# Split projection weights kept in DRAM by the first block, and the elementwise chain spread over the r and v units

## The chip, the cores and the metric

The kernel runs on one core of one Trainium2 chip. The metric is the time of one execution on the device in microseconds (us). One execution of each kernel is also recorded by the hardware profiler. Engines are named as in the profile: PE is TensorE (PEld its weight loads), DVE is VectorE, ACT is ScalarE, POOL is GpSimd, SP is SyncE, which here only issues DMAs.

## What is computed

Two layers on 2048 latent tokens with 256 context tokens as a prefix, 1024 channels: a bidirectional RWKV-7 mixer, then latent attention, each with modulated norms, a gate and a residual. The change is inside the projections of the RWKV mixer:

```python
def rwkv_prepare(h, mu, w_in, w0, w1, w2, a0, a1, a2, k_k, k_a):
    xx = centred_shift(h)
    lerp = lambda j: h + xx * mu[j]
    r = heads(lerp(0) @ w_in[0])
    k = heads(lerp(1) @ w_in[1])
    v = heads(lerp(2) @ w_in[2])
    gate = lerp(3) @ w_in[3]
    ...
    logw = heads(-jnp.exp(-jax.nn.softplus(-wpre) - 0.5))
    a = heads(jax.nn.sigmoid(...))
    kk = ...  # k * k_k, normalised per head
    k_dir = k[None] * (1.0 + (a - 1.0) * k_a.reshape(RWKV_HEADS, RWKV_HEAD))
    b = kk[None] * a
    return r, logw, k_dir, v, -kk, b, gate
```

`wpre` and `a` are there once for each of two directions; everything downstream of them is done twice.

## The kernel before

`run` goes through parameters, `project`, `scan` and `attention`. `project` calls `project_block` for five blocks of tokens: the context (256 columns, block 0) and four of 512 (blocks 1 to 4). Channels lie on partitions, in 8 tiles (index f for outputs, k for inputs); tokens are columns.

The large products run in split precision. `lerp_split(j)` makes the 8 input tiles of `lerp(j)` (L480) and parts each into a rounded half `lh` (L492, ACT) and the rest `ll` (L493, DVE, or POOL for odd k with j of 0 and 1). `load_w` does the same to a weight tile `wraw` of 128x1024: `whi` is a cast on ACT (L414), `wlo` the difference (L418), on POOL or parted between DVE and POOL by `DVK`, `DVR` and `DVV`. `mm3` then issues 24 matmuls (L500 to L502). All 24 tiles (k, r, v, 8 each) are loaded from the input and split again in every block. `w_seq` gives the order of the loads; one load runs ahead.

A block of 512 columns has these stretches: 16 fp32 matmuls for the low-rank hidden layers (L520); the **k units**, 8 times `load_w`, `mm3`, copies and a lerp kept for the gate; the **r units**, 8 times `mm3`, and for each two **halves** (direction d of 0 and 1); the **v units**, 8 times `mm3`, transposes and stores, with the norm of the next block (`pr_norm`) and steps of a small triangular solve (L1002, L1006, blocks 1 and 2) between them. In block 0 each v unit follows its r unit.

A half takes 4 matmuls `w2` (L602, L603) into `ps_l`, two tanh on ACT (`sg`, `ta`), then on DVE `sg`+1 (L610), a scan along the tokens (L613), two exponentials on ACT (`E`, `Ei`), and products that make `ar` (L622, L623, DVE), `kd` (L627, POOL), the first part of `kb` (L630, POOL), `ta` (L631, DVE) and the second part of `kb` (L632, DVE). `ar` and `kb` are stored by SP, 512 KB each; 32 small matmuls `ab` (L641) use them. Once for each f DVE makes `kkh` (L591) and `bt` (L657), and POOL adds the two `kd` (L655).

The order on each engine is set by the framework's scheduler from this program and from the buffers of its pools; engines run their own lists in order and wait for one another by semaphores. SP issues nearly all DMAs, in one list.

Of the kernel before, what the change touches and what calls it, by code (L numbers as in the profile page):

```python
# [19 lines left out]
P = 128  # L20
# [101 lines left out]
class Build:  # L122
# [194 lines left out]
    def project(self):  # L317
# [3 lines left out]
        with ExitStack() as es:  # L321
# [4 lines left out]
            tags = itertools.cycle(((wp, "whi"), (wp, "wlo"), (tp, "ar")))  # L326

            def modw():
                pool, tag = next(tags)
                return pool.tile([P, D], F32, name="modw", tag=tag, bufs=2)  # L330

            mg = self.mod_gen([(0, 0, 512, D)], 5, tp, pp, modw, "ps_l", {"tag": "kkh"})
# [10 lines left out]
            self.w_raw = next(self.w_it)  # L343
# [47 lines left out]
    def w_seq(self, wp):  # L391
        nc, ins = self.nc, self.ins
        for t0, _ in BLOCKS:
            for w1 in ("rwkv_w1", "rwkv_a1"):
                raw = wp.tile([P, KT, P], F32, name="wraw")
                for d in range(2):
                    nc.sync.dma_start(raw[:, :, d * 64:(d + 1) * 64], ins[w1][0, d].rearrange("(k p) m -> p k m", p=P))
                yield raw
            order = [(1, f) for f in range(KT)]
            order += [(j, f) for j in (0, 2) for f in range(KT)] if t0 else [(j, f) for f in range(KT) for j in (0, 2)]  # L400
            for j, f in order:
                raw = wp.tile([P, KT, P], F32, name="wraw")
                nc.sync.dma_start(raw, ins["rwkv_w_in"][0, j, :, f * P:(f + 1) * P].rearrange("(k p) m -> p k m", p=P))
                yield raw

    def next_raw(self):
        cur, self.w_raw = self.w_raw, next(self.w_it, None)
        return cur

    def load_w(self, wp, dv=0):  # L410
        nc = self.nc
        raw = self.next_raw()
        hi = wp.tile([P, KT, P], F32R, name="whi")
        nc.scalar.copy(hi, raw)  # L414
        lo = wp.tile([P, KT, P], F32R, name="wlo")
        for eng, k0, k1 in ((nc.vector, 0, dv), (nc.gpsimd, dv, KT)):
            if k1 > k0:
                eng.tensor_tensor(lo[:, k0:k1, :], raw[:, k0:k1, :], hi[:, k0:k1, :].bitcast(F32), ALU.subtract)  # L418
# [52 lines left out]
    def project_block(self, t0, W, bp, wp, tp, pp, ind, indt, smask, w2d, sol):  # L471
# [6 lines left out]
        def lerp(j, k):  # L478
            L = tp.tile([P, 512], F32, name="lerp", bufs=4)
# [3 lines left out]
        def lerp_split(j, into=None):  # L483
            lh, ll = [], []
            for k in range(KT):
# [3 lines left out]
                else:  # L489
                    h = bp.tile([P, 512], F32R, name="lh", bufs=10)  # L490
                    l = bp.tile([P, 512], F32R, name="ll", bufs=9)
                nc.scalar.copy(h[:, :W], L[:, :W])  # L492
                (nc.gpsimd if k % 2 and j != 2 else nc.vector).tensor_tensor(l[:, :W], L[:, :W], h[:, :W].bitcast(F32), ALU.subtract)  # L493
# [19 lines left out]
        DVK, DVR, DVV = (5, 0), (2, 0), (5, 3)  # L513
        HS = []
        for j in (4, 5):
            raw = self.next_raw()
            ps = pp.tile([P, 512], F32, name="ps_r")
            for k in range(KT):
                L = lerp(j, k)
                nc.tensor.matmul(ps[:, :W], raw[:, k, :], L[:, :W], start=k == 0, stop=k == KT - 1)  # L520
# [13 lines left out]
        for f in range(KT):  # L534
            hi, lo = self.load_w(wp, DVK[t0 > 0])
# [21 lines left out]
        def v_unit(f, lh, ll):  # L557
# [4 lines left out]
            hi, lo = self.load_w(wp, DVV[t0 > 0])  # L562
# [18 lines left out]
        bts = []  # L581
        abq = []
        for f in range(KT):
            hi, lo = self.load_w(wp, DVR[t0 > 0])
            if f == 0:
                w2 = load_w2(0)
            pi = pp.tile([P, 512], F32, name="ps_i", bufs=1)
            nc.tensor.matmul(pi[:, :W], indt[:, f, :], ivh[:, :W], start=True, stop=False)
# [1330 lines left out]
```

## Time and profile before

| | |
|---|---|
| runs | 5359.62, 5360.29, 5380.01 us; median 5360.29 us |
| profiled execution | 5361.62 us, its span 5359.8 us |
| mean granted TensorE clock | 0.92 of full speed |
| busy over the span | PE 86%, DVE 70%, POOL 54%, ACT 40% |
| the projection | from the start to about 1322 us |

The span is what the profiler saw from the first to the last instruction; 1.8 us lie around it. Busy shares are means over stages with different limits. The projection has its own pattern, which is why the rows below are taken from stretches of it.

### The profile page before, as it was taken

The page shows a single profiled execution, that of the slowest core. Times are in us where ns is not written, and L with a number is a line of the kernel's source. Part 1 is how long each engine was busy: PE and PEld are TensorE (multiplying, and loading weights), DVE is VectorE, ACT ScalarE, POOL GpSimd, SP SyncE. Part 2 cuts the span into 40 slices and gives each one's busy share as a digit, 9 for nine tenths or more (in the row PEclk, how much of TensorE's full clock was granted, in tenths as well). Part 3 has the DMA queues.
Part 4 walks back from the last instruction along what each step waited for, and adds up shares of the span by engine and source line. Part 5 has one row for each costly group of instructions (what it writes and reads, how often), then busy time and mean ns, then how long its engine had stood idle before and what let it go on. Part 6 is the DMA issues. An engine that isn't in the chain of part 4 may idle for free. (4 is left out here: it accounts for less than half of the span.)

```text
span 5359.8 us, 122473 instructions
## 1 busy us (share of the span) xinstructions
PE 4623.4 (86%) x50175; PEld 3437.2 (64%) x50175; DVE 3726.7 (70%) x6054; ACT 2167.4 (40%) x3830; POOL 2885.2 (54%) x2539
## 2 busy tenths in 40 slices
PE   6788788887878888677879999869999999999999
PEld 4555555555667777556757777746666666666667
DVE  5989898886788888777655544336666776666634
ACT  4544444443444444333433334214343434343332
POOL 2575656464454444434244444227777777777751
PEclk8898888888889899788979999979999999999999
DMA  7655464646776666877878777761111111211023
GB/s 220 190 167 174 151 182 153 188 152 188 211 219 183 182 175 182 219 212 223 243 228 259 240 216 192 237 213 34 60 58 33 57 54 34 60 58 34 27 94 107
DMA packets 1006877, 818.53 MB, mean 153 GB/s; under 512 B 280885, under 2 KB 876420, under 8 KB 994794
## 3 DMA queue, kind: packets, MB, share of 16 engines
q1 hardware_dynamic: 872046, 734.48, 46.0%
q10 hardware_dynamic: 134188, 75.95, 5.2%
q8 instruction: 394, 6.46, 0.5%
q14 instruction: 169, 1.38, 0.1%
q0 software_dynamic: 80, 0.26, 0.0%
HBM read 551.84 MB, written 258.66 MB: 151 GB/s over the span
## 5 line engine op out<-in xcount | busy, mean ns | idle before, releaser
L1724 POOL TENSOR_TENSOR acc<-acc,pt 128x1024 f32<-128x1024 f32 x416 | 1003.1, 2411 | 356.3 <-ACT pt L1712 333.6
L1712 ACT ACTIVATE pt<-ps_s 128x1024 f32<-128x1024 f32 x576 | 590.9, 1027 | 890.3 <-PE ps_s L1710 882.8
L1690 DVE TENSOR_REDUCE mx<-ps_p 128x1 f32<-128x512 f32 x1024 | 659.6, 686 | 258.6 <-PE ps_p L1686 258.6
L1731 PE MATMUL ps_o<-pt,av 128*64 128x512 f32 x2304 | 514.0, 595 | 0.0
L1710 PE MATMUL ps_s<-qr,a_kr 64*128 64x512 f32 (+1 forms) x2304 | 474.2, 392 | 0.3 <-DVE qr L1701 0.2
L418 POOL TENSOR_TENSOR wlo<-wraw,whi 128x1024 fp32r<-128x1024 f32 (+3 forms) x120 | 261.7, 2181 | 299.7 <-ACT whi L414 290.0
L500 PE MATMUL ps_r<-lh,whi 128*128 128x512 f32 (+1 forms) x960 | 384.6, 403 | 38.0 <-ACT lh L492 34.7
L501 PE MATMUL ps_r<-ll,whi 128*128 128x512 f32 (+1 forms) x960 | 381.6, 399 | 16.5 <-DVE ll L493 13.4
L502 PE MATMUL ps_r<-lh,wlo 128*128 128x512 f32 (+1 forms) x960 | 378.4, 396 | 15.0 <-DVE wlo L418 7.6
L696 POOL TENSOR_TENSOR f_wlo<-f_wraw,f_whi 128x384 fp32r<-128x384 f32 x118 | 159.3, 1350 | 388.6 <-ACT f_whi L694 339.8
L1731 PEld LDWEIGHTS ps_o<-pt,av 128*64 128x64 f32 x2304 | 159.5, 137 | 315.5 <-issue 315.5
L1686 PE MATMUL ps_p<-knh,qnh 64*128 64x512 f32 (+1 forms) x1280 | 274.7, 399 | 37.4 <-DMA qnl<-qn 33.3
L480 DVE SCALAR_TENSOR_TENSOR lerp<-xx,cols,hb 128x512 f32<-128x512 f32 (+1 forms) x240 | 239.2, 1022 | 86.1 <-POOL ll L493 65.9
L1150 PE MATMUL ps_s<-svu,big 128*64 128x64 f32 x4544 | 235.3, 247 | 50.9 <-DVE svu L1138 27.8
L1110 ACT COPY big<-ps_aa 64x256 f32<-64x256 f32 x576 | 211.0, 366 | 131.0 <-PE ps_aa L1106 125.0
L1097 DVE TENSOR_TENSOR big<-ps_aa,amask 64x256 f32<-64x256 f32 x576 | 243.0, 422 | 28.5 <-PE ps_aa L1092 15.0
L1686 PE MATMUL ps_p<-a_kr,qr 64*128 64x512 f32 (+1 forms) x1280 | 260.4, 379 | 1.7 <-DMA qr<-qr 1.7
L1710 PEld LDWEIGHTS ps_s<-qr,a_kr 64*128 64x128 f32 (+1 forms) x2304 | 235.2, 185 | 38.4 <-DVE qr L1701 0.5
L500 PEld LDWEIGHTS ps_r<-lh,whi 128*128 128x128 f32 x960 | 197.7, 206 | 92.3 <-ACT lh L492 39.4
L1710 PE MATMUL ps_s<-qnh,knl 64*128 64x512 f32 x1152 | 241.0, 402 | 12.2 <-ACT pt L1712 12.0
L1150 PEld LDWEIGHTS ps_s<-svu,big 128*64 128x64 f32 x4544 | 193.9, 156 | 86.0 <-DVE svu L1138 40.9
L501 PEld LDWEIGHTS ps_r<-ll,whi 128*128 128x128 f32 x960 | 198.0, 206 | 59.6 <-DVE ll L493 19.7
(343 smaller groups left out, 12357.4 us busy)
## 6 DMA issues: line engine op xcount, KB each, us to landing
f_w<-wod SPq DMA_DIRECT2D x72, 1024.0 KB
wraw<-rwkv_w_in SPq DMA_DIRECT2D x120, 512.0 KB
kbt<-KB SPq DMA_DIRECT2D x72, 512.0 KB
big<-AR SPq DMA_DIRECT2D x144, 256.0 KB
AR<-ar SPq DMA_DIRECT2D x64, 512.0 KB
KB<-kb SPq DMA_DIRECT2D x64, 512.0 KB
f_wraw<-rwkv_w_in SPq DMA_DIRECT2D x64, 512.0 KB
f_wraw<-mla_w_in SPq DMA_DIRECT2D x54, 512.0 KB
```

The costliest lines, as they stand in the source:

```text
L418: eng.tensor_tensor(lo[:, k0:k1, :], raw[:, k0:k1, :], hi[:, k0:k1, :].bitcast(F32), ALU.subtract)
L500: nc.tensor.matmul(ps, hi[:, k, :], lh[k][:, :W], start=k == 0, stop=False)
L501: nc.tensor.matmul(ps, hi[:, k, :], ll[k][:, :W], start=False, stop=False)
L502: nc.tensor.matmul(ps, lo[:, k, :], lh[k][:, :W], start=False, stop=k == KT - 1)
L1097: nc.vector.tensor_tensor(B[r, 2 * p0 + e::4, 0, ck], ps[e][o], amask[o, d:d + 1, :].to_broadcast([64, 4, 64]), ALU.mult)
L1150: nc.tensor.matmul(ps[e * 64:(e + 1) * 64, h // 2, :], B[:, h, 1, k:k + 64], S[:, e, h // 2, :], start=True, stop=True)
L1686: nc.tensor.matmul(ps[h2][:, o * kw:(o + 1) * kw], x[r, t * P:(t + 1) * P], y[r, k0:k0 + kw], start=st, stop=not st)
L1690: nc.vector.tensor_reduce(mx[:, h2, t, n % 4:n % 4 + 1], ps[h2], mybir.AxisListType.X, ALU.max)
L1710: nc.tensor.matmul(ps[:, h2, :], x[r, ks], y[r, :], start=i == 0, stop=i == 4)
L1712: nc.scalar.activation(pt, ps, AF.Exp, scale=SCALE)
L1724: eng.tensor_tensor(a, a, pt, ALU.add)
L1731: nc.tensor.matmul(st["po"][hs, :], st["v"][:, kt, hs], pt[:, h2, :], start=kt == 0, stop=kt == NK - 1)
```

## The change

`w_seq` and `load_w`: in block 0 a weight tile is split as before, in `w`, a buffer that holds both halves (1 MB), and `w` is stored to a DRAM tensor `wid`. Blocks 1 to 4 load both halves from `wid`, 1 MB for each unit, up to two units ahead. The raw tile, the split pair, the tile of low-rank weights and the modulation weights share three buffers of 1 MB. `project_block`: all r units stand before all v units in block 0 too; each of the 16 units is followed by one half (`elem`) in place of two in each r unit, and ACT copies r from PSUM to `rt` (five buffers), which the halves read. In the halves all products are on DVE. The `ll` of odd k goes to DVE as well. `lh` and `ll` have 8 buffers (10 and 9 before), `lerp` 3 (4 before), and `Ei` is written over `cs`.

```diff
 def w_seq(self, wp):
...
+            for j in (1, 0, 2):
+                for f in range(KT):
+                    if t0:
+                        w = wp.tile([P, 2, KT, P], F32R, name="w", bufs=3)
+                        nc.sync.dma_start(w.rearrange("p i k m -> p i (k m)").bitcast(F32), self.wid[j, f].bitcast(F32))
+                    else:
+                        w = wp.tile([P, 2, KT, P], F32, name="wraw", tag="w", bufs=3)
+                        nc.sync.dma_start(w[:, 0], ins["rwkv_w_in"][0, j, :, f * P:(f + 1) * P].rearrange("(k p) m -> p k m", p=P))
+                    yield w
...
+    def load_w(self, wp, t0, j, f):
         nc = self.nc
+        raw = self.next_w(2 if t0 else 1)
+        if t0:
+            return raw[:, 0], raw[:, 1]
+        w = wp.tile([P, 2, KT, P], F32R, name="w", bufs=3)
+        hi, lo = w[:, 0], w[:, 1]
+        nc.scalar.copy(hi, raw[:, 0])
+        dv = (2, 5, 5)[j]
         for eng, k0, k1 in ((nc.vector, 0, dv), (nc.gpsimd, dv, KT)):
+            eng.tensor_tensor(lo[:, k0:k1, :], raw[:, 0, k0:k1, :], hi[:, k0:k1, :].bitcast(F32), ALU.subtract)
+        nc.sync.dma_start(self.wid[j, f].bitcast(F32), w.rearrange("p i k m -> p i (k m)").bitcast(F32))
         return hi, lo
...
-                (nc.gpsimd if k % 2 and j != 2 else nc.vector).tensor_tensor(l[:, :W], L[:, :W], h[:, :W].bitcast(F32), ALU.subtract)
+                nc.vector.tensor_tensor(l[:, :W], L[:, :W], h[:, :W].bitcast(F32), ALU.subtract)
...
+        def r_unit(f):
+            hi, lo = self.load_w(wp, t0, 0, f)
...
+            mm3(psr[:, :W], hi, lo, lh, ll)
+            rt = tp.tile([P, 512], F32, name="rt", bufs=5)
+            nc.scalar.copy(rt[:, :W], psr[:, :W])
...
+        def elem(f, d, st={}):
...
+            nc.vector.scalar_tensor_tensor(ta[:, :W], ta[:, :W], 1.0, kkh[:, :W], ALU.add, ALU.mult)
+            nc.vector.tensor_tensor(kd[:, :W], kd[:, :W], kT[:, f, :W], ALU.mult)
...
+            nc.vector.tensor_tensor(rc(kb[:, :nch, 32:64]), chunked(ta[:, :W]), chunked(Ei[:, :W]), ALU.mult)
+            nc.vector.tensor_tensor(kb[:, :nch, 0:32], chunked(kd[:, :W]), chunked(Ei[:, :W]), ALU.mult)
...
+                nc.vector.tensor_tensor(s[:, :W], s[:, :W], kd[:, :W], ALU.add)
...
+        for u in range(2 * KT):
+            if u < KT:
+                r_unit(u)
+            else:
+                if u == KT and t0:
+                    lv = lerp_split(2)
+                v_unit(u - KT, *lv)
             if abq:
+                ab()
+            elem(u // 2, u % 2)
```

The scheduler lays the lists out anew. On DVE, in the r units of block 2, one half and the step to the next f read like this before (the scan is printed as a SCALAR_TENSOR_TENSOR into `cs`):

```order
L610 TENSOR_SCALAR sg<-sg 128x512
L613 SCALAR_TENSOR_TENSOR cs<-c_smask,sg 128x512
L631 SCALAR_TENSOR_TENSOR ta<-ta,kkh 128x512
L622 SCALAR_TENSOR_TENSOR ar<-kkh,E 128x16x32
L623 TENSOR_TENSOR ar<-ps_r,E 128x16x32
L632 TENSOR_TENSOR kb<-ta,Ei 128x16x32
L657 SCALAR_TENSOR_TENSOR sq<-kd_6172,cols_111,ps_r 128x512
L591 SCALAR_TENSOR_TENSOR kkh<-kT,cols_111,ps_i 128x512
```

The same place of DVE's list after the change, the second half of an f and the step to the next:

```order
L628 TENSOR_SCALAR sg<-sg 128x512
L631 SCALAR_TENSOR_TENSOR cs<-c_smask,sg 128x512
L641 SCALAR_TENSOR_TENSOR ta<-ta,kkh 128x512
L642 TENSOR_TENSOR kd_5965<-kd_5965,kT 128x512
L655 TENSOR_TENSOR kd_5865<-kd_5865,kd_5965 128x512
L645 SCALAR_TENSOR_TENSOR ar<-kkh,E 128x16x32
L646 TENSOR_TENSOR ar<-rt,E 128x16x32
L649 TENSOR_TENSOR kb<-ta,cs 128x16x32
L650 TENSOR_TENSOR kb<-kd_5965,cs 128x16x32
L657 SCALAR_TENSOR_TENSOR sq<-kd_5865,cols_111,rt 128x512
L613 SCALAR_TENSOR_TENSOR kkh<-kT,cols_111,ps_i 128x512
```

Three operations, L642, L655 and L650, have come over from POOL's list; the `sq` row (`bt` in the program) and `kkh` stand between this half's last product and the next half's `sg`.

SP's list in the k units of block 0 after the change (`wid` is the DRAM tensor, `w` a split pair, `L3` the lerp kept for the gate):

```order
L431 DMA wid_158<-w_521 128x2048
L409 DMA wraw_563<-rwkv_w_in 128x8x128
L557 DMA L3_65<-lerp_694 128x256
L557 DMA L3_65<-lerp_737 128x256
L557 DMA L3_65<-lerp_777 128x256
L523 DMA w2s_918<-w2d_145 128x1024
L431 DMA wid_158<-w_565 128x2048
L409 DMA wraw_609<-rwkv_w_in 128x8x128
```

Each unit now has a store of its pair ahead of the next raw load, where before the loads of `wraw` and the stores of `L3` followed each other alone.

## Rows read from the trace of the kernel before

**Rows 1.** First line of the page.
```profile
span 5359.8 us, 122473 instructions
```
**Rows 2.** Busy by stretch; columns: from:to, length, engines' busy (instructions), granted clock, DMA share, GB/s.
```profile
68.20:105.30 37.10, 32.41 (x206) 27.48 (x207) 23.65 (x35) 19.96 (x38) 19.54 (x14) 0.86 0.75 219
105.30:230.00 124.70, 89.91 (x976) 78.49 (x974) 113.38 (x191) 69.52 (x161) 66.58 (x86) 0.86 0.68 199
...
308.60:506.50 197.90, 153.86 (x1565) 112.51 (x1563) 182.10 (x217) 91.98 (x160) 127.92 (x119) 0.88 0.62 191
590.40:788.20 197.80, 152.68 (x1563) 111.80 (x1561) 181.19 (x215) 90.06 (x157) 126.83 (x118) 0.86 0.63 192
865.00:1058.70 193.70, 153.01 (x1563) 112.91 (x1561) 172.10 (x185) 89.95 (x157) 106.36 (x87) 0.87 0.62 193
1134.90:1322.00 187.10, 148.72 (x1531) 109.84 (x1528) 144.73 (x147) 81.18 (x143) 106.41 (x83) 0.86 0.58 183
```
**Rows 3.** DVE by line, r units of block 2: count, shortest/median/longest ns, starts.
```profile
L610 DVE TENSOR_SCALAR sg<-sg x13: 411/1290/2121, 619.4 to 716.0; 128x512 f32<-128x512 f32 x13
L613 DVE TENSOR_TENSOR_SCAN cs<-c_smask,sg x13: 1208/2280/2315, 620.0 to 716.9; 128x512 f32<-128x512 f32 x13
L631 DVE SCALAR_TENSOR_TENSOR ta<-ta,kkh x14: 660/1504/1794, 610.1 to 711.1; 128x512 f32<-128x512 f32 x14
L622 DVE SCALAR_TENSOR_TENSOR ar<-kkh,E x14: 690/694/1940, 609.5 to 712.3; 128x512 f32<-128x512 f32 x14
L623 DVE TENSOR_TENSOR ar<-ps_r,E x14: 629/678/684, 604.9 to 712.9; 128x512 f32<-128x512 f32 x14
L632 DVE TENSOR_TENSOR kb<-ta,Ei x14: 677/1180/2825, 613.5 to 713.5; 128x512 f32<-128x512 f32 x14
L591 DVE SCALAR_TENSOR_TENSOR kkh<-kT,cols,ps_i x8: 733/734/748, 608.7 to 715.3; 128x512 f32<-128x512 f32 x8
L493 DVE TENSOR_TENSOR ll<-lerp,lh x7: 676/679/1773, 588.7 to 716.3; 128x512 fp32r<-128x512 f32 x7
```
**Rows 4.** Timeline, two scans in block 2: start, length, engine, line, operation.
```profile
651.79 1.23 DVE L613 TENSOR_TENSOR_SCAN cs<-c_smask,sg 128x512 f32<-128x512 f32 x1
...
658.25 1.71 POOL L627 TENSOR_TENSOR kd<-kd,kT 128x512 f32<-128x512 f32 x1
658.75 2.29 DVE L613 TENSOR_TENSOR_SCAN cs<-c_smask,sg 128x512 f32<-128x512 f32 x1
```
**Rows 5.** Timeline of the handover between two halves, block 2.
```profile
648.14 0.68 ACT L607 ACTIVATE sg<-ps_l,w0h 128x512 f32<-128x512 f32 x1
...
649.29 0.76 PE L641 MATMUL ps_ab<-ar,kb 64*32 64x32 f32 x64 [1.17 <-DVE kb L632]
...
650.31 0.39 PE L603 MATMUL ps_l<-hs,w2s 128*128 128x512 f32 x1
```
**Rows 6.** DVE in the v units of block 2: one line of the next block's norm.
```profile
L457 DVE TENSOR_TENSOR xx<-xx,rs_r x8: 677/922/2054, 751.3 to 762.4; 128x512 f32<-128x512 f32 x8
```
**Rows 7.** Sum over the k units of blocks 1 to 4: length, then busy by engine.
```profile
sum 250.50, PE 219.36 PEld 156.07 DVE 182.95 ACT 116.62 POOL 161.25; mean PE 54.84 PEld 39.02 DVE 45.74 ACT 29.16 POOL 40.31
```
**Rows 8.** Who waited for `wlo` in the k units of block 3 (us, times).
```profile
  PE ps_r L502: 3.4, 2
```
**Rows 9.** Timeline of a load and a split in the k units of block 0.
```profile
78.94 0.38 SPq L403 DMA_DIRECT2D wraw<-rwkv_w_in  x1
...
83.68 1.05 ACT L414 CAST whi<-wraw 128x1024 fp32r<-128x1024 f32 x1 [1.63 <-DMA wraw<-rwkv_w_in]
...
84.80 1.65 POOL L418 TENSOR_TENSOR wlo<-wraw,whi 128x384 fp32r<-128x384 f32 x1 [3.88 <-ACT whi L414]
```
**Rows 10.** POOL's part of the splits in the r and v units of block 0, ns.
```profile
L418 POOL TENSOR_TENSOR wlo<-wraw,whi x16: 1004/1732/2077, 104.2 to 223.9; 128x768 fp32r<-128x768 f32 x8, 128x384 fp32r<-128x384 f32 x8
```
**Rows 11.** Busy by stretch as in rows 2: part of the scan, r units of block 2.
```profile
2200.00:2250.00 50.00, 34.20 (x838) 23.03 (x838) 34.02 (x80) 15.02 (x37) 19.03 (x34) 0.74 0.97 245
590.40:718.00 127.60, 95.35 (x1181) 68.05 (x1178) 119.84 (x115) 63.00 (x114) 89.58 (x74) 0.84 0.60 194
```

More of the change, by code (lines that the diff above doesn't have):

```diff
@@ L325, in project @@
             pp = es.enter_context(tc.tile_pool(name="pr_ps", bufs=2, space=PSUM))
-            tags = itertools.cycle(((wp, "whi"), (wp, "wlo"), (tp, "ar")))
+            halves = []
             def modw():
-                pool, tag = next(tags)
-                return pool.tile([P, D], F32, name="modw", tag=tag, bufs=2)
-            mg = self.mod_gen([(0, 0, 512, D)], 5, tp, pp, modw, "ps_l", {"tag": "kkh"})
+                if not halves:
+                    w = wp.tile([P, 2, D], F32, name="modw", tag="w", bufs=3)
+                    halves.extend((w[:, 0], w[:, 1]))
+                return halves.pop(0)
+            self.wid = self.scrr("wid", [3, KT, P, 2, KT * P])
+            mg = self.mod_gen([(0, 0, 512, D)], 4, tp, pp, modw, "ps_l", {"tag": "kkh"})
             self.pr_load(bp, 0)
@@ L400, in w_seq @@
[L400 to L410, printed above, removed]
-        nc = self.nc
[L412 to L415, printed above, removed]
+                    nc.sync.dma_start(w[:, i, :, d * 64:(d + 1) * 64], ins[w1][0, d].rearrange("(k p) m -> p k m", p=P))
@@ L580, in project_block @@
         pb = pp.tile([P, 512], F32, name="ps_s", bufs=1)
[L581 to L584, printed above, removed]
+        rts, bts, abq = [], [], []
+        w2s = {}
+        def r_unit(f):
+            hi, lo = self.load_w(wp, t0, 0, f)
             if f == 0:
-                w2 = load_w2(0)
-            pi = pp.tile([P, 512], F32, name="ps_i", bufs=1)
-            nc.tensor.matmul(pi[:, :W], indt[:, f, :], ivh[:, :W], start=True, stop=False)
-            nc.tensor.matmul(pi[:, :W], indt[:, f, :], ivl[:, :W], start=False, stop=True)
-            kkh = tp.tile([P, 512], F32, name="kkh")
-            nc.vector.scalar_tensor_tensor(kkh[:, :W], kT[:, f, :W], col["kk"][:, f:f + 1], pi[:, :W], ALU.mult, ALU.mult)
+                w2s[0] = load_w2(0)
@@ new lines, in ab @@
+        def ab():
+            f, d, kb, ar = abq.pop(0)
+            lab = tp.tile([P, 4, 2, 32], F32, name="lab")
+            for e in range(2):
+                r = slice(e * 64, (e + 1) * 64)
+                pab = pp.tile([P, 4, 32], F32, name="ps_ab")
+                for c in range(nch):
+                    g = slice(32 * (c % 4), 32 * (c % 4) + 32)
+                    nc.tensor.matmul(pab[g, c // 4 if d == 0 else nch // 4 - 1 - c // 4, :], kb[r, c, 32:64], ar[r, c, 0:32], start=True, stop=True)
+                nc.scalar.copy(lab[:, :nch // 4, e, :], pab[:, :nch // 4, :])
+            cls, q = (2 * f) % 4, f // 2
+            n0 = self.natb(d, c0 // 4 if d == 0 else c0 // 4 + nch // 4 - 1)
+            dst = self.Ld[n0:n0 + nch // 4].rearrange("b (k z q g) (s t) -> q k z b (g s) t", k=4, z=2, q=4, s=32)
+            for e in range(2):
+                nc.scalar.dma_start(dst[q, cls + e, d].rearrange("b w t -> w b t"), lab[:, :nch // 4, e, :])
```

158 lines of the change are left out of this document (70 added, 88 removed).

## Prediction

> **What bounds the kernel now.** The page comes first, for the span of 5359.8 us [rows 1]; the profiled execution took 5361.6 us, 1.8 us around it, and is 1.3 us above the median of the runs, 5360.3 us. The change touches the projection alone, so the next view is the busy time by stretch, cut at the first and last matmuls of the k units and of the r and v units. The reader is to see two kinds of stretch. In the r and v units of blocks 1 to 3 (193.7 to 197.9 us each) DVE is busy 172 to 182 us and PE 153 us [rows 2]: DVE sets the pace, PE waits. In the k units of blocks 1 to 4 (250.5 us together) PE is busy 219.4 us [rows 7]: PE sets the pace.
>
> Then the same DVE operations, line by line, in the r units of block 2. One operation on one shape has lengths far apart: the scan 1208 ns at the shortest and 2280 ns at the median, `sg`+1 411 and 1290, `ta` 660 and 1504, `kb` 677 and 1180; the operations that read PSUM (`kkh`, the second `ar`) hardly vary [rows 3]. The timeline shows what goes with it: a scan with no POOL operation beside it took 1.23 us, one that began during POOL's `kd` product took 2.29 us [rows 4]. So a good part of DVE's 182 us is time in which it stands beside a running POOL operation.
>
> **The change part by part.**
>
> *The r and v units of blocks 1 to 4.* POOL loses its products, and the splits too, which are gone in these blocks. I therefore price DVE's operations at their shortest. One half: 0.411 + 1.208 + 0.660 + 0.690 + 0.629 + 0.677 = 4.28 us [rows 3]. Added: `kd` and the first part of `kb`, priced as the other part of `kb`, 2 x 0.677 = 1.35 us. Half of what comes once for each f (`kkh` 0.733, `bt` priced the same, the sum of the `kd` 0.677) is 1.07 us. Together 6.70 us a half, 107.2 us a block.
>
> Beside it DVE has two `lerp_split`s, 8 x (0.733 + 0.676) = 11.3 us each, the lerp priced as `kkh` [rows 3]; 8 copies of v at 0.68 = 5.4 us; and in blocks 1 to 3 the next block's norm, 24 operations at 0.68 [rows 6] and 4 at 0.73, 19.2 us. Blocks 1 and 2 hold the steps of the solve, which I read as the difference between blocks 2 or 1 and block 3, 182.1 - 172.1 = 10 us [rows 2]. The floor of DVE is 107.2 + 22.6 + 5.4 + 19.2 + 10 = 164.4 us in blocks 1 and 2, 154.4 in block 3, 135.2 in block 4.
>
> DVE will not reach that floor. The `ab` matmuls of a half wait for its last `kb`; the next half's `w2` matmuls stand behind them on PE, then its tanh on ACT, then its `sg` on DVE. From the rows of one handover: `ab` began at 649.29, the second of the `w2` matmuls that feed `sg` ended at 650.70, and the tanh takes 0.68 us [rows 5]: 2.1 us, with the semaphores about 2.2. On DVE only `bt` and `kkh` (1.47 us, after every second half) stand in that gap, as DVE's list shows. A pair of r halves is then 2 x 6.70 + 2 x 2.2 - 1.47 = 16.3 us, four pairs 65 us. The first r unit waits for its lerps and the inverse of the norms, 13 us (11.3 and something over); of the second `lerp_split` 3 us go into such gaps, 8 remain. In the v units the norm, the solve and the copies fill the gaps; I leave 0.5 us a unit: 8 x (6.70 + 0.68 + 0.5) = 63 us, plus 19.2 and 10 where they are. Block 4 has no norm to fill them: 8 x (6.70 + 0.68) + 8 x (2.2 - 0.68 - 0.73) = 65 us. Sums: blocks 1 and 2 13 + 65 + 8 + 92 = 178 us against 197.9 and 197.8, block 3 168 against 193.7, block 4 151 against 187.1 [rows 2]: **-101 us**. The ends: at DVE's floor -158 us; with the whole handover of 2.2 us in each of 16 units and nothing in it, the four blocks come to 200, 200, 190 and 170 us, -17 us.
>
> *The k units of blocks 1 to 4.* Casts and subtractions go; the pair comes by DMA. What PE can win is its idle 250.5 - 219.4 = 31 us at most [rows 7], most of it the wait for the first lerps, which stay. In block 3 its wait for `wlo` alone was 3.4 us [rows 8]; four times that is 14 us, so **-14 us**, between 0 and -31. The `ll` of odd k moved to DVE costs 4 x 0.676 = 2.7 us there before the first k unit, but POOL's version is waited for too, so I price it at nothing; its cover is that wait, and without it 4 x 2.7 = 11 us come back, inside these ends.
>
> *Block 0.* Here the change costs. Three buffers hold the raw tile, the raw tile after it and one split pair, so a unit's cast waits until the pair before has been used and has landed in `wid`. No such store is in the trace. In the r units of block 2 the DMA engines moved 194 GB/s at a share of 0.60 [rows 11], 323 GB/s when busy; 1.05 MB is then 3.24 us at least. A raw load of half the size, among other transfers, took from its issue at 78.94 to 83.68, 4.74 us [rows 9]; with the other half's 1.62 us that is 6.4 us. I take 5.0 us, nearer the upper row since stores of `ar` and `kb` share the queue. A k unit: cast 1.05, POOL's part of the subtraction 1.65 [rows 9], store 5.0 = 7.7 us, 8 of them 62 us against 37.1 [rows 2]. An r unit, with POOL's larger part at 2.08 [rows 10], is 8.1 us, a v unit 7.7: together 127 us against 124.7. **+27 us.** With 3.24 us the k units take 48 us and the others fall to about 114 us, where DVE is busy now, 0 in all; with 6.4 us it is 73 us and 149 us, +60.
>
> The Trainium skill, "DMA: Bandwidth & Descriptors", section on the anatomy of one DMA, fits a DMA as 2.0 us and the bytes at 436 GB/s, which would make the store 4.4 us and, as an estimate from that page, block 0 cost 12 us in place of 27; the load of [rows 9] took longer than that fit gives for its size, so the rows decide.
>
> *Buffers and queues.* A pair for blocks 1 to 4 is asked for when a buffer comes free, two units before its use, over 13 us in the k units (PE is busy 219.4 / 32 = 6.9 us a unit [rows 7]); a store of `ar` or `kb` waiting on DVE holds SP's list behind it, but DVE is at most one half behind PE. I price that at nothing; what it costs if transfers are slow is a rival. `lh` and `ll` with 8 buffers hold the first `lerp_split` of the r units back until the last k unit has begun; that lies in the 13 us. The copy to `rt` is on ACT, half idle [rows 2].
>
> The sum: 5361.6 - 101 - 14 + 27 = 5273.6 us, against the median 1.3 less, **5272 us**.
>
> **The rivals.** *(a) DVE is full and gets more to do: slower.* If DVE's operations keep their present lengths, the products moved to it add 16 x 1.35 + 8 x 0.677 + 4 x 0.677 = 29.8 us a block to a DVE that is busy 182 of 198 us. With a rest of 10 us for handovers blocks 1 to 4 take 222, 221, 212 and 185 us, +63; with the gain in the k units spent on DVE's longer lerps and +27 in block 0 the time is about 5451 us. It decides where a half costs over 8.0 us in place of 6.70: (101 + 14 - 27) / 64 = 1.4 us more and the gain is gone. For it speaks that POOL keeps the solve and the small `E` operations; against it the scan at 1.23 us with POOL idle [rows 4] and the shortest lengths of [rows 3].
>
> By the Trainium skill, "Perfetto Trace Analysis", section on Scalar and DVE operations, a saturated DVE is to be relieved to ScalarE or even GpSimd, the reverse of this change; the same passage warns that moving between those two might not help. The trace bears out the warning. I give rival (a) 0.08.
>
> *(b) The transfers become the bound: no change.* A block's r and v units move 16.8 MB of pairs, 16.8 of `ar` and `kb`, 4.2 of `w2s`, 2.1 each of the `ab` results, v in two forms and the next x, and 1 of low-rank weights, 47 MB: 146 us at 323 GB/s, under the 151 to 178 above. In the scan's heaviest stretch the rate was 245 GB/s at a share of 0.97 [rows 11], 253 GB/s; at that rate it is 187 us a block, and the sum is -11 -11 -7 - 0 - 14, with +45 for block 0: 5363 us. For it: the margin is small. Against: the r units of block 2, with half of these transfers, ran at 323 GB/s. 0.07.
>
> *(c) Block 0 and the handovers eat most of it: no change.* Block 0 at its +60 and the four blocks at -17 and -14 give 5391 us, so both would have to be near their worse ends for no gain; partly so, at +45, -55 and -14, it is 5338 us. 0.07 within 0.5%.
>
> **How the numbers follow.** 0.5%, 27 us, is about what a measurement of this kernel can tell from no change. The forecast is the likeliest, 0.78, and holds all that is faster by more; rivals (b) and (c) make 0.14 for no change; (a) 0.08 for slower. Ends of the terms alone reach from -158 - 31 = 5172 us to -17 + 60 = 5405 us. For 8 in 10 I take about two thirds of the better end, 5205 us, and at the worse end what takes in (c) at halfway, 5345 us; (a) and the far half of (b) are left out.
>
> **What would show it.** Right: in the r and v units of blocks 1 to 4 the scan near 1.21 us at the median, a pair of r halves near 16 us, those stretches at 151 to 178 us; the four k stretches near 59 us each in place of 62.6, PE not waiting for a split; block 0's k units near 62 us, ACT waiting there for the store into `wid`. Wrong: DVE's lengths as before (rival a); PE waiting for `w` from `wid` with a DMA share over 0.9 (rival b); block 0 longer by over 45 us, or DVE idle more than 2 us a unit through the v units as well (rival c); a longer start of the scan after the last v unit, which I have not priced since its list is the same.

## The result, and the profile after

The changed kernel takes 5284.8 us (median of 4 runs, 5278.9 to 5285.8) against 5362.8 us for the kernel before, timed beside it (4 runs, 5359.6 to 5380.0): a ratio of 0.985, 95% interval 0.983 to 0.986. It is 1.5% faster; 5272 us was forecast, in a range of 5205 to 5345. The profiled run took 5278.9 us. First line of its page, which answers to [rows 1]:

```profile
span 5277.1 us, 122006 instructions
```

The stretches, cut as in [rows 2] (columns as there): block 0's k units, its r and v units, then the r and v units of blocks 1 to 4.

```profile
78.90:148.60 69.70, 46.28 (x224) 38.33 (x224) 28.74 (x56) 26.66 (x54) 13.43 (x10) 0.77 0.74 234
148.60:315.60 167.00, 112.50 (x983) 94.51 (x984) 98.54 (x209) 66.26 (x146) 39.25 (x46) 0.74 0.77 243
385.60:536.10 150.50, 133.75 (x1424) 99.89 (x1422) 131.81 (x216) 82.42 (x147) 37.22 (x58) 0.99 0.84 275
622.90:772.70 149.80, 132.31 (x1416) 98.64 (x1414) 126.79 (x208) 75.74 (x137) 36.05 (x56) 0.98 0.84 273
857.40:1005.50 148.10, 134.45 (x1417) 102.13 (x1414) 119.27 (x185) 76.54 (x137) 12.12 (x28) 0.94 0.86 275
1088.70:1232.30 143.60, 130.69 (x1388) 99.69 (x1386) 107.62 (x161) 66.78 (x123) 12.41 (x27) 0.94 0.81 266
```

The reader is to see two movements against each other. In blocks 1 to 4 the stretch falls from between 187 and 198 us to between 143 and 151 us, and VectorE's busy time falls with it, although three products were added to it. In block 0 both stretches grow, from 37.1 to 69.7 and from 124.7 to 167.0 us.

The k units of blocks 1 to 4, which answer to [rows 7] (the sum of the four stretches):

```profile
sum 203.10, PE 200.45 PEld 147.32 DVE 127.82 ACT 89.67 POOL 30.50; mean PE 50.11 PEld 36.83 DVE 31.95 ACT 22.42 POOL 7.62
```

They took 250.5 us with TensorE busy 219.4; now TensorE is busy 200.45 of 203.1 us. VectorE by line in the r and v units of block 2, as in [rows 3]:

```profile
L628 DVE TENSOR_SCALAR sg<-sg x13: 411/417/428, 651.7 to 772.1; 128x512 f32<-128x512 f32 x13
L631 DVE TENSOR_TENSOR_SCAN cs<-c_smask,sg x12: 1208/1224/1225, 652.2 to 761.0; 128x512 f32<-128x512 f32 x12
L641 DVE SCALAR_TENSOR_TENSOR ta<-ta,kkh x14: 666/680/991, 635.5 to 760.4; 128x512 f32<-128x512 f32 x14
L649 DVE TENSOR_TENSOR kb<-ta,cs x14: 674/682/985, 636.7 to 765.4; 128x512 f32<-128x512 f32 x14
L642 DVE TENSOR_TENSOR kd<-kd,kT x13: 678/683/973, 653.9 to 772.4; 128x512 f32<-128x512 f32 x13
```

The medians stand at the shortest lengths of before: the scan 1.22 in place of 2.28 us, `sg`+1 0.42 in place of 1.29, `ta` 0.68 in place of 1.50.

The last cut needs care. Before, the next block's first low-rank matmul followed the last v matmul at once (788.2 and 788.4 us for block 2). Now the chain of the last half stands between them:

```profile
782.51 1.22 DVE L631 TENSOR_TENSOR_SCAN cs<-c_smask,sg 128x512 f32<-128x512 f32 x1
...
788.52 0.75 DVE L657 SCALAR_TENSOR_TENSOR sq<-kd,cols,rt 128x512 f32<-128x512 f32 x1
...
791.19 1.22 PE L532 MATMUL ps_r<-lerp,w 128*128 128x512 f32 x1
```

From 772.7 to 791.2 are 18.5 us that this stretch hands on. So stages that follow one another without a gap are compared from here on, cut at the first low-rank matmul (L532 here) and at the first r matmul of each block (us, profiled runs):

| stage | before | after | moved | forecast |
|---|---|---|---|---|
| start, to block 0's first low-rank matmul | 54.9 | 65.1 | +10.2 | 0 |
| block 0, to block 1's | 175.7 | 250.7 | +75.0 | +27 |
| low-rank and k stage, blocks 1 to 4 | 314.4 | 271.1 | -43.3 | -14 |
| r and v stage, blocks 1 to 3 | 590.1 | 501.8 | -88.3 | -65 |
| r and v stage of block 4 and all behind it | 4224.9 | 4188.4 | -36.5 | -36 |
| span | 5359.8 | 5277.1 | -82.7 | -88 |

The last row but one also holds the scan and the attention, whose code is the same. From block 4's last store to the end, that part took 4030.8 to 4052.9 us in the profiles of the changed kernel and of those below that keep the spread, so differences under some 20 us in that row say little.

### The profile page after: what moved, and what is told of

It reads as the page before. It is cut to its first block, busy times and chain, and to the rows that moved or that the text cites. A ratio compares the mean times of both kernels' runs of the same rounds, so it can differ in the third digit from the quotient of the medians.

```text
span 5277.1 us, 122006 instructions
## 1 busy us (share of the span) xinstructions
PE 4593.6 (87%) x50175; PEld 3431.7 (65%) x50175; DVE 3529.0 (67%) x6262; ACT 2112.0 (40%) x3774; POOL 2360.6 (45%) x2203
## 5 line engine op out<-in xcount | busy, mean ns | idle before, releaser
L513 PE MATMUL ps_r<-lh,w 128*128 128x512 f32 (+1 forms) x960 | 379.7, 400 | 36.0 <-ACT w L427 34.2
L515 PE MATMUL ps_r<-lh,w 128*128 128x512 f32 (+1 forms) x960 | 379.7, 396 | 15.2 <-DVE w L430 13.5
L514 PE MATMUL ps_r<-ll,w 128*128 128x512 f32 (+1 forms) x960 | 378.1, 394 | 4.0 <-DVE ll L506 3.7
L1752 PEld LDWEIGHTS ps_o<-pt,av 128*64 128x64 f32 x2304 | 159.6, 137 | 315.5 <-issue 315.5
L638 POOL COPY EC<-E 128x16 f32<-128x16 f32 (+1 forms) x80 | 77.0, 964 | 552.3 <-ACT E L635 546.7
L513 PEld LDWEIGHTS ps_r<-lh,w 128*128 128x128 f32 x960 | 200.4, 210 | 92.1 <-ACT w L427 42.1
L1731 PE MATMUL ps_s<-qnh,knh 64*128 64x512 f32 x1152 | 240.4, 389 | 0.0
L1731 PE MATMUL ps_s<-qnl,knh 64*128 64x512 f32 x1152 | 240.3, 392 | 0.0
```

Source lines behind the costliest of these rows:

```text
L513: nc.tensor.matmul(ps, hi[:, k, :], lh[k][:, :W], start=k == 0, stop=False)
L514: nc.tensor.matmul(ps, hi[:, k, :], ll[k][:, :W], start=False, stop=False)
L515: nc.tensor.matmul(ps, lo[:, k, :], lh[k][:, :W], start=False, stop=k == KT - 1)
L1731: nc.tensor.matmul(ps[:, h2, :], x[r, ks], y[r, :], start=i == 0, stop=i == 4)
L1752: nc.tensor.matmul(st["po"][hs, :], st["v"][:, kt, hs], pt[:, h2, :], start=kt == 0, stop=kt == NK - 1)
```

## The experiments

The theory after the first profile: POOL's products made VectorE's own operations longer, and taking them away is the gain; the weights in DRAM gain in blocks 1 to 4 and cost in block 0, where one pair buffer and the stores hold the units up. The kernels below were timed in three sets; the kernel before took 5367.5, 5369.8 and 5368.3 us in them.

### The products back on POOL

```diff
-            nc.vector.tensor_tensor(kd[:, :W], kd[:, :W], kT[:, f, :W], ALU.mult)
+            nc.gpsimd.tensor_tensor(kd[:, :W], kd[:, :W], kT[:, f, :W], ALU.mult)
...
-            nc.vector.tensor_tensor(kb[:, :nch, 0:32], chunked(kd[:, :W]), chunked(Ei[:, :W]), ALU.mult)
+            nc.gpsimd.tensor_tensor(kb[:, :nch, 0:32], chunked(kd[:, :W]), chunked(Ei[:, :W]), ALU.mult)
...
-                nc.vector.tensor_tensor(s[:, :W], s[:, :W], kd[:, :W], ALU.add)
+                nc.gpsimd.tensor_tensor(s[:, :W], s[:, :W], kd[:, :W], ALU.add)
```

> The changed kernel with the three products (kd by kT, the kd half of kb, the sum of both kd) back on POOL; weights from DRAM and the spread stay. Theory C (POOL's elementwise work makes VectorE's own operations longer): in blocks 1 to 3 the scan's median goes from 1.21 back to about 2.2 us and sg + 1 from 0.42 to about 1.2, VectorE loses 1.7 us of products a half but pays about 3 us in longer operations, the r and v units go from 150 us to 160 to 175 in each block, and the time is 5320 to 5370 us. Theory D (the gain is the spread's and the weights', the place of the products is worth nothing): the blocks stay within 5 us, 5275 to 5300 us.

Measured: 5369.2 us, ratio 1.000 (0.999 to 1.001): in sum the whole gain is gone, 84 us. Theory C holds, but for one point, and D falls. The whole r and v stage of block 2 in the changed kernel (columns as in [rows 2]):

```profile
622.90:791.20 168.30, 140.41 (x1566) 102.29 (x1563) 145.25 (x242) 82.22 (x149) 41.12 (x62) 0.95 0.85 276
```

The same stage with the products back on POOL, and three of its VectorE operations:

```profile
646.10:828.40 182.30, 151.29 (x1508) 113.73 (x1505) 159.62 (x204) 86.08 (x153) 93.09 (x99) 0.91 0.73 235
```

```profile
L631 DVE TENSOR_TENSOR_SCAN cs<-c_smask,sg x15: 1211/1224/2326, 656.4 to 820.0; 128x512 f32<-128x512 f32 x15
L641 DVE SCALAR_TENSOR_TENSOR ta<-ta,kkh x15: 659/955/1795, 660.5 to 821.1; 128x512 f32<-128x512 f32 x15
L646 DVE TENSOR_TENSOR ar<-rt,E x14: 676/798/1776, 659.9 to 811.6; 128x512 f32<-128x512 f32 x14
```

VectorE gave up 40 operations of 0.68 us (two products in each of 16 halves, eight sums), some 27 us by their recorded lengths, and is yet busy 159.6 us in place of 145.3, so its other operations grew by about 41 us. The stage is 14.0 us longer, as much as VectorE's busy time grew. That POOL's slower products hold up the chain itself would be a rival; but VectorE waited for POOL only once in this stage, 1.2 us, and its idle time is 23 us in both kernels. One point of the expectation failed: the scan's median stayed at 1.22 us (only its longest is 2.3). In this order of the chain `ta`, both parts of `ar` and `kb` stand beside the products. The timeline shows how:

```profile
758.37 1.79 POOL L642 TENSOR_TENSOR kd<-kd,kT 128x512 f32<-128x512 f32 x1 [0.52 <-ACT kd L640]
...
758.92 1.78 DVE L641 SCALAR_TENSOR_TENSOR ta<-ta,kkh 128x512 f32<-128x512 f32 x1
...
760.24 1.63 POOL L650 TENSOR_TENSOR kb<-kd,cs 128x512 f32<-128x512 f32 x1
...
760.81 1.60 DVE L649 TENSOR_TENSOR kb<-ta,cs 128x512 f32<-128x512 f32 x1
```

`ta` began during POOL's product and ended at 760.70, 0.54 us after POOL's end at 760.16; alone it takes 0.66. `kb` ended 0.54 us after POOL's second product. The Trainium skill, "SBUF — State Buffer", section "Who interferes with whom", says that a VectorE instruction with two SBUF inputs and a GpSimd instruction that reads SBUF exclude each other for a whole instruction, and that one with a single SBUF input, outside the modes that use both ports, is not touched. The trace agrees within 0.15 us on the first; on the second, the second `ar`, which read `ps_r` in PSUM in the kernel before, took at most 0.68 us there [rows 3], and up to 1.78 us here, where it reads the SBUF copy `rt`. `sg`+1 has a single SBUF input and was held all the same (0.41 us at the shortest and 1.29 at the median before [rows 3]), so the exception for these modes matters; in which mode it ran no run shows.

"Gone" is a sum of two movements. In the profile of this kernel blocks 1 to 4 and all behind them are 89 us shorter than before the change (of these 57 in the r and v stages of blocks 1 to 3), and the start and block 0 are 92 us longer.

### The products alone, in the kernel before

The same three edits in the kernel before.

> The kernel before with one edit: the three products (kd by kT, the kd half of kb, the sum of both kd) on VectorE in place of POOL. Theory L (the products are worth their 84 us in any kernel): 5367 - 84, about 5285 us, as the whole change. Theory M (here POOL still splits the weights of every unit, some 2 us beside VectorE's chain, and both halves stand in the r unit, which VectorE sets): an r unit loses the lengthening by POOL's products and gains 3.4 us of products, the r and v stages of blocks 1 to 3 go from 198 to about 184 us, 55 us in all, about 5312 us (5295 to 5330). Rival N (VectorE is full there and each product comes on top, 8 x 3.4 us a block): slower, 5367 + 4 x 27, about 5470 us.

Measured: 5308.0 us, ratio 0.989 (0.987 to 0.990), -60 us. The time is theory M's; N, which is the prediction's rival (a) without the rest of the change, is far off. By stage M fits less well: the r and v stages of blocks 1 to 3 take 189.5, 184.6 and 182.9 us where it had 184, which is 33 of the 55 us between the two profiles, and 11 more lie in the k stages, which the edit does not touch. Its scan in the r and v units of block 2:

```profile
L613 DVE TENSOR_TENSOR_SCAN cs<-c_smask,sg x14: 1209/1212/1522, 600.3 to 688.0; 128x512 f32<-128x512 f32 x14
```

So one of the edit's three parts gives 60 of the 78 us. Weights and spread without the products (the kernel of the section before) give nothing in sum, for block 0 takes what blocks 1 to 4 gain; with the products they add some 18 us more.

### The spread undone in blocks 1 to 4

```diff
-        for u in range(2 * KT):
+        for u in range(KT if t0 else 2 * KT):
...
-            if abq:
-                ab()
-            elem(u // 2, u % 2)
+            for f, d in ((u, 0), (u, 1)) if t0 else ((u // 2, u % 2),):
+                if abq:
+                    ab()
+                elem(f, d)
...
+        if t0:
+            lv = lerp_split(2)
+            for f in range(KT):
+                v_unit(f, *lv)
```

> The changed kernel, but in blocks 1 to 4 both halves of the elementwise chain stand in the r unit again and the eight v units follow without any; block 0 is as in the changed kernel. Theory E (the spread lets TensorE and VectorE overlap over the whole stage): r units are bound by VectorE's pair of halves, 8 x 16.0 = 128 us, then the lerps of v, about 8 us, and eight v units by TensorE, 8 x 5.5 = 44 us: 180 us in place of 167 in each block, 10 to 16 us more in each of four, 5325 to 5350 us. Theory F (VectorE's sum sets the stage however it is spread, the gain came from the products alone): within 5 us a block, 5275 to 5300 us.

Measured: 5304.8 us, ratio 0.988 (0.986 to 0.990), 20 us behind the changed kernel: between the two theories. The r and v stages of blocks 1 to 3 take 173.7, 172.8 and 172.0 us against 169.0, 168.3 and 164.5, 5.6 us a block and not 13. Theory E's terms were off on both sides: from the first r matmul to the end of the first v unit, which waits for the last half, it is 126.6 us (384.1 to 510.7 in block 1) where E had 128 + 8 and a unit; the seven units that follow take 6.8 us each with their gaps, not 5.5. The gain of the spread is the smaller for the 18.5 us that TensorE waits at the block's end with it.

### The weights split again in every block

No weights in DRAM: raw loads, cast on ACT, subtraction mostly on POOL.

```diff
-                    if t0:
-                        w = wp.tile([P, 2, KT, P], F32R, name="w", bufs=3)
-                        nc.sync.dma_start(w.rearrange("p i k m -> p i (k m)").bitcast(F32), self.wid[j, f].bitcast(F32))
-                    else:
-                        w = wp.tile([P, 2, KT, P], F32, name="wraw", tag="w", bufs=3)
+                    if (t0, j, f) == (0, 1, 0):
+                        self.rawbuf = wp.tile([P, 2, KT, P], F32, name="wraw", tag="w", bufs=3)
+                        n = 0
+                    w = self.rawbuf[:, n % 2:n % 2 + 1]
+                    n += 1
...
-        dv = (2, 5, 5)[j]
+        dv = ((0, 3, 0) if t0 else (2, 5, 5))[j]
...
-        nc.sync.dma_start(self.wid[j, f].bitcast(F32), w.rearrange("p i k m -> p i (k m)").bitcast(F32))
```

> The changed kernel without the weights in DRAM: every block loads the raw weights and splits them again (cast on ACT; in blocks 1 to 4 the subtraction on POOL, in the k units 3 of 8 slices on VectorE; two pair buffers, two raw halves). Spread and products on VectorE stay. Block 0 then loses its 24 stores and the single pair buffer: 250.7 us to about 186, as the kernel without the stores has it. Theory G (the loads save more than the split's own time, for POOL's split lies beside VectorE's chain): the k stages of blocks 1 to 4 go from 50.8 to about 60 us each and the r and v units from 148 to about 160, some 22 a block, 88 in all, against 64 saved in block 0: about 5310 us (5290 to 5340). Theory H (with the products off POOL the split fits beside the rest): blocks 1 to 4 stay within 5 us each, about 5225 us (5215 to 5245), and the weights in DRAM are a loss as they stand.

Measured: 5314.5 us, ratio 0.990 (0.988 to 0.991); theory G, with both of its terms larger than it had them. Block 0 takes 175.7 us, exactly as before the change, 75.0 less than with the stores. In exchange the k stages take 296.2 us in place of 271.1, the r and v stages of blocks 1 to 3 561.3 in place of 501.8, and block 4 and all behind it 26 more. The k units of block 1 here (columns as in [rows 2]):

```profile
255.70:314.40 58.70, 52.94 (x214) 38.17 (x213) 45.98 (x80) 30.03 (x46) 26.44 (x30) 0.97 0.35 108
```

The first 24 of its matmuls take 13.8 us; with pairs from DRAM they take 8.3. The weights in DRAM are worth 30 us net as made, an estimated 105 us if block 0 were free (30 and the 75).

### Two pair buffers in block 0, and no stores

What holds block 0? The changed kernel's timeline in its k units, and the chief waits of block 0 (us, times, longest):

```profile
114.57 1.64 POOL L430 TENSOR_TENSOR w<-wraw,w 128x384 fp32r<-128x384 f32 x1 [7.01 <-ACT w L427]
...
116.23 0.32 SPq L431 DMA_DIRECT2D wid<-w  x1
...
121.40 1.04 ACT L427 CAST w<-wraw 128x1024 fp32r<-128x1024 f32 x1 [1.01 <-DMA wid<-w]
```

```profile
PEld ps_r L513 <- ACT w L427: 42.1, 20, 5.2
PE ps_r L513 <- ACT w L427: 34.2, 16, 4.9
```

The store was issued at 116.23 and let the next cast go at 121.40: 5.2 us; 5.0 was priced. Two kernels take the hold away in two ways. The first gives the raw tiles one buffer of two halves, and so the pairs two:

```diff
-                        w = wp.tile([P, 2, KT, P], F32, name="wraw", tag="w", bufs=3)
+                        if (j, f) == (1, 0):
+                            self.rawbuf = wp.tile([P, 2, KT, P], F32, name="wraw", tag="w", bufs=3)
+                            n = 0
+                        w = self.rawbuf[:, n % 2:n % 2 + 1]
+                        n += 1
```

> The changed kernel, but in block 0 the raw weight tiles take turns in the two halves of one buffer, so that the split pairs have two buffers in place of one; everything else is as in the changed kernel (5284.8 us). Theory A (the one pair buffer holds block 0 up: the next unit's cast waits until TensorE has used the pair and the store has landed): the k units of block 0 go from 69.7 us to about 45 (8 x 5.5), its r and v units from 167.0 to about 130, the wait of the cast on TensorE and the store (now 42 + 34 us at the other end, TensorE waiting for the cast) falls under 20 us, and the time is about 5225 us (5205 to 5245). Theory B (block 0 is held by its transfers, by the split itself or by the slower clock): block 0 stays within 15 us, 5270 to 5290 us.

The second leaves 21 of 24 stores out:

```diff
-                        nc.sync.dma_start(w.rearrange("p i k m -> p i (k m)").bitcast(F32), self.wid[j, f].bitcast(F32))
+                        nc.sync.dma_start(w.rearrange("p i k m -> p i (k m)").bitcast(F32), self.wid[j, 0].bitcast(F32))
...
-        nc.sync.dma_start(self.wid[j, f].bitcast(F32), w.rearrange("p i k m -> p i (k m)").bitcast(F32))
+        if f == 0:
+            nc.sync.dma_start(self.wid[j, f].bitcast(F32), w.rearrange("p i k m -> p i (k m)").bitcast(F32))
```

> The changed kernel with only the first split pair of each projection kept in DRAM; the blocks 1 to 4 load that pair for all eight units of the projection (as many bytes, wrong weights, so the output is another). Left out: 21 of the 24 stores of 1 MB in block 0. Theory S (the landing of the store is what keeps the pair buffer): each of the 24 units of block 0 loses about 3 us, the time falls by 60 to 75 us to about 5215. Theory P (TensorE's own use of the pair keeps it, the store lands beside it): only the 12.7 us in which the cast was seen waiting for the store go, about 5270 us (5262 to 5285), and the units of block 0 stay over 7.5 us (k) and 9.5 us (r and v).

Measured: 5268.1 us with two pair buffers, ratio 0.981 (0.978 to 0.983), and 5235.4 us without the stores, 0.975 (0.973 to 0.978). Block 0's two stretches, with two pair buffers:

```profile
75.10:124.30 49.20, 38.13 (x208) 30.48 (x208) 26.20 (x45) 19.22 (x40) 11.11 (x7) 0.86 0.82 276
124.30:289.80 165.50, 109.11 (x1000) 92.31 (x1001) 111.41 (x228) 73.65 (x166) 37.74 (x48) 0.74 0.80 256
```

and without the stores, with the one pair buffer:

```profile
78.00:127.60 49.60, 37.17 (x224) 29.87 (x224) 25.95 (x51) 23.39 (x48) 13.38 (x10) 0.91 0.58 181
127.60:255.10 127.50, 95.71 (x954) 79.90 (x954) 102.64 (x209) 66.18 (x150) 38.52 (x46) 0.84 0.68 201
```

In the k units both cures give the same, 49 us, 20 less. That does not make the store's landing the only hold there. The kernel that splits again in every block has neither: no stores and two pair buffers. Its k units of block 0:

```profile
75.60:111.40 35.80, 32.97 (x209) 27.57 (x210) 22.81 (x40) 18.78 (x38) 10.94 (x8) 0.90 0.58 173
```

So with the stores gone the one pair buffer, held by TensorE's use of it alone, still costs 14 us (49.6 against 35.8), and with two pair buffers the stores still cost 13 (49.2 against 35.8): both holds are real. In the r and v units the second buffer gives nothing beside the stores, and the stores are 40 us. Neither theory A nor B, nor S nor P, holds for the whole block; the two stretches have different limits.

### The r and v units of block 0: the queue, or the transfers

The first kernel here also gives the start its six tiles of modulation weights again; the second adds a later place for the store.

```diff
-                    w = wp.tile([P, 2, D], F32, name="modw", tag="w", bufs=3)
-                    halves.extend((w[:, 0], w[:, 1]))
+                    for _ in range(2):
+                        w = wp.tile([P, 2, D], F32, name="modw", tag="w", bufs=3)
+                        halves.extend((w[:, 0], w[:, 1]))
+                    for _ in range(2):
+                        halves.append(tp.tile([P, D], F32, name="modx", tag="ar", bufs=2))
...
-            mg = self.mod_gen([(0, 0, 512, D)], 4, tp, pp, modw, "ps_l", {"tag": "kkh"})
+            mg = self.mod_gen([(0, 0, 512, D)], 5, tp, pp, modw, "ps_l", {"tag": "kkh"})
```

> The kernel with two pair buffers in block 0 (5268.1 us), and the rows of the modulation weights ahead of block 0 have six tiles again, loaded five ahead, in place of four and four. Theory I (the 10.2 us by which the first lora matmul came later are those missing tiles): the first lora matmul starts at about 55 us in place of 64.5, the rest stays, about 5258 us (5250 to 5268). Rival (the ten microseconds are the raw weights' and constants' place in the queue): the start stays at 62 to 66 us and the time at 5268.

Measured: 5266.8 us, ratio 0.981 (0.979 to 0.983). The first low-rank matmul starts at 59.5 us, not 55 and not 62 to 66: about half of the ten microseconds were the tiles. Its time cannot be told from that with two pair buffers alone.

```diff
         raw = self.next_w(2 if t0 else 1)
+        if not t0 and self.pend:
+            self.pend()
...
-        nc.sync.dma_start(self.wid[j, f].bitcast(F32), w.rearrange("p i k m -> p i (k m)").bitcast(F32))
+        self.pend = lambda: nc.sync.dma_start(self.wid[j, f].bitcast(F32), w.rearrange("p i k m -> p i (k m)").bitcast(F32))
```

> As the kernel with two pair buffers and six modulation tiles, but the store of a pair in block 0 is issued a unit later, behind the next raw load, when the split is long done, so that nothing on SP's queue waits behind it. Theory J (in block 0's r and v units SP's queue is held by the store that waits for its split, and the w2 load, the stores of AR and KB and the next raw load behind it): r and v of block 0 go from 165.5 us to about 140, the time falls by 20 to 30 us, about 5232 us. Theory K (the transfers themselves are the bound there, 0.78 of the engines' time at 258 GB/s): r and v stay at 158 to 170 us, within 8 us of the run beside it.

Measured: 5253.1 us, ratio 0.979 (0.977 to 0.980), the fastest kernel here that leaves nothing out, 32 us under the changed kernel. But block 0 gained only 6.4 us of the 20 to 30 that theory J wanted. (The two profiles differ by 26.6 us; 22 of them lie in the r and v stages of blocks 1 to 3 and of block 4 and behind, whose program the edit leaves alone.) Its r and v units stay long:

```profile
123.30:283.20 159.90, 105.14 (x975) 88.89 (x976) 103.51 (x216) 70.01 (x158) 34.94 (x47) 0.73 0.79 258
```

Their first to last matmul are 164.6 us against 168.9 in the run beside it, which is theory K's figure. It rules out the one order that theory J named, and not the order as such: SP still stands 30.5 us in this stretch waiting for VectorE's `kb`. Two more kernels take stores away from there. One keeps only the k pairs in DRAM (`if j == 1` around the store, and the raw path for r and v in every block):

> As the kernel with two pair buffers and six modulation tiles, but only the k weights are kept in DRAM; r and v weights are split again in each block, by ACT and POOL. Block 0 loses 16 of 24 stores: its r and v units go from 165.5 to about 130 us, its k units stay at 49. Theory G: POOL's split in the r and v units of blocks 1 to 4 lengthens VectorE's operations, 148 to about 160 us a block, 48 in all: no gain, about 5265 to 5280 us. Theory H: these blocks stay within 5 us each, about 5222 us (5210 to 5240).

Measured: 5286.8 us, ratio 0.985 (0.983 to 0.986). Block 0's r and v units fall to 123.7 us, as expected, but the stages of blocks 1 to 3 take 186.0, 188.1 and 179.9 us in place of 171, 168 and 167: theory G, a little beyond its range. The gain is spent. The other keeps the v pairs one block later (store `if (j == 2) == bool(t0)`):

> The kernel with two pair buffers, six modulation tiles and the later store (5253.1 us), with the v pairs kept one block later: block 0 splits the v weights without storing them, block 1 loads them raw, splits them again (ACT and POOL) and stores them, the blocks 2 to 4 load them. Theory K (transfers are the bound of block 0's r and v units): the last eight units there go from 82 to about 64 us; block 1's r and v units pay 5 to 12 us for the split beside VectorE's chain; about 5243 us (5235 to 5255). Rival (block 0's v units are bound by the chain of cast, split and matmul on one unit after another): the last eight units stay within 4 us, and block 1's price makes it 5255 to 5268 us.

Measured: 5273.1 us, ratio 0.982 (0.980 to 0.984). The last eight units of block 0 go from 83.7 to 66.5 us, what theory K gave, but block 1's stage pays 24 us (188.3 against 164.3), twice the most that was expected, and the lost time between the blocks 8 more, so the kernel is 20 us slower. That stores are the limit of those units is shown three times; whether by the rate of the DMA engines or by the order on SP's one queue stays open. A share of 0.79 at 258 GB/s is not the 0.97 of [rows 11]; but the mix of transfers differs, so that does not settle it.

## Why the prediction was right, and where it was not

**The mechanism was right and shown.** VectorE's operations came to the shortest lengths that [rows 3] listed, a pair of r halves takes 15.5 to 16.0 us (three pairs, from the first `kkh` to the fourth, 46.5 to 48.0 in the four blocks) against 16.3 forecast, and with the products back on POOL `ta`, both parts of `ar` and `kb` grew again and the stage of block 2 became 14.0 us longer. Rival (a), 5451 us, needed VectorE at its old lengths; none of the operations that had been long kept its median.

**The total was right because two mis-sized terms cancelled, which is luck.** The gains in blocks 1 to 4 were 168 us, not 115; block 0 and the start cost 85 us, not 27.

- *r and v units, -101:* measured -125. The step that failed is "DVE will not reach that floor", in the v units. The stage of block 2, cut where the first eight halves end (the fourth `sq`, 700.0), columns as in [rows 2]:

```profile
622.90:700.00 77.10, 69.76 (x771) 53.18 (x768) 58.98 (x88) 36.22 (x67) 8.64 (x14) 0.96 0.77 262
700.00:791.20 91.20, 70.65 (x796) 49.12 (x795) 86.28 (x155) 46.00 (x83) 32.47 (x49) 0.94 0.93 287
```

  The first eight halves took 77.1 us, as forecast (13 + 65), with the handover gaps in them. The other eight took 91.2 where the prediction had 8 + 92 = 100: there VectorE is busy 86.3 of 91.2 us, the gaps filled by the norm, the copies and the next half. And 164.4 us was no floor, for VectorE is busy 145 us in the whole stage (some of its records are missing). It added up recorded lengths, and neighbouring records overlap:

```profile
741.74 0.68 DVE L641 SCALAR_TENSOR_TENSOR ta<-ta,kkh 128x512 f32<-128x512 f32 x1
742.34 0.69 DVE L642 TENSOR_TENSOR kd<-kd,kT 128x512 f32<-128x512 f32 x1
```

- *k units, -14, at most -31:* measured -43 with the low-rank stages, -47 in the k stretches alone. The step that failed is "most of it the wait for the first lerps, which stay". The first 24 matmuls of the four k stretches, before and after:

```profile
sum 57.65, PE 40.52 PEld 25.27 DVE 57.27 ACT 34.02 POOL 36.12; mean PE 10.13 PEld 6.32 DVE 14.32 ACT 8.51 POOL 9.03
sum 31.62, PE 29.51 PEld 19.75 DVE 31.25 ACT 24.45 POOL 13.79; mean PE 7.38 PEld 4.94 DVE 7.81 ACT 6.11 POOL 3.45
```

  They are 26 us shorter together, 15 of it TensorE's idle time and 11 its busy time, at a granted clock of 0.80 to 0.92 before and 1.00 after; with the split done again in each block they take 55.2. TensorE's wait there was indeed for the lerps' halves, and for `wlo` 1.1 us a block at most. But POOL's split held these too. In block 1 of the kernel before:

```profile
255.07 2.79 POOL L418 TENSOR_TENSOR wlo<-wraw,whi 128x1024 fp32r<-128x1024 f32 x1
...
255.69 3.32 DVE L493 TENSOR_TENSOR ll<-lerp,lh 128x512 fp32r<-128x512 f32 x2
...
258.47 0.79 PE L501 MATMUL ps_r<-ll,whi 128*128 128x512 f32 x1 [3.72 <-DVE ll L493]
```

  The first of these two `ll` was done only 0.6 us after POOL's end at 257.86: the contention that the prediction read in the r units was here as well. It went with the split; in the changed kernel no `ll` took over 0.88 us there. And the bound was none: it took TensorE's busy time as fixed, and that fell by 19 us over the k stretches, at a granted clock of 1.00 in all four where it had been 0.94, 0.90, 0.94 and 0.94.
- *Block 0, +27:* measured +75. In the k units the store was priced about right (5.0 priced, 5.2 in the one measured), but the unit became 8.7 us, not 7.7: the sum has no term for TensorE's use of the one pair buffer, which is worth 14 us over the eight units where the stores are gone. The section of the Trainium skill, "DMA: Bandwidth & Descriptors", that the prediction quotes gives its fit for transfers that GpSimd issues. These stores are SyncE's, and the 4.4 us beside the price was no price for them. The larger step that failed is "an r unit ... is 8.1 us, a v unit 7.7: together 127 us against 124.7". Without the stores these units took 127.5 us, what the prediction gave them with the stores, and with them 167.0: the stores come on top of what `ar`, `kb`, `w2s` and raw weights already move. TensorE, waiting between the units, also had its clock at 0.74 there in place of 0.86, and was busy 112.5 us for the work of 89.9.
- *The start, unpriced:* +10. "The same list" was true of the scan, not of the modulation weights, which had lost two of six tiles; giving them back brought half of it back.
- *Rival (b), transfers:* not in blocks 1 to 4. Block 2 moved 287 GB/s at a share of 0.93 in its last eight halves (the row from 700.0 above), and yet TensorE's weight loads waited for pairs from `wid` for 2.9 us in all four blocks together. In block 0, where the prediction allowed +45, the stores cost 40 us in the r and v units alone; whether as transfers stays open. *Rival (c)* named block 0's +60 and the handovers; the first came and more; the handovers came in the r units, as priced, and hardly in the v units.

## What to carry to other kernels

Before giving an engine that is busy all the time more work, look whether its operations have two lengths and which other engine runs in the long ones: here work that made another engine's operations wait was cheaper on the engine that waited. Do not add up recorded lengths to a floor without looking whether they overlap. Price a store of an intermediate in the stage that writes it, with everything that shares its queue, and not by its landing alone; then look which buffer it holds, and who else holds that buffer. When several edits go together, run each alone: here one of three gave 60 of 78 us, and the other two gave nothing in sum without it. And read "nothing" by stage: it was 89 us gained and 92 lost.

## What the runs showed of the hardware

- Three products taken off VectorE made it busier: 145.3 to 159.6 us in block 2's r and v stage, for 40 operations of 0.68 us less.
- Moving an operand from PSUM to SBUF exposes an operation to POOL: the second `ar` went from at most 0.68 us to up to 1.78 us.
- The same matmuls of a stretch in the k units kept TensorE busy 219.4 us with waits between them and 200.5 us without, the granted clock being 0.90 to 0.94 in the four stretches and 1.00 in all of them: there a gap was paid twice, as the wait and in the clock.
